# The state-space scan of a three-block layer stack: TensorE's order written out, decays two steps ahead, between-block decays from a table

## The chip, the cores and the metric

One core of one Trainium2 chip. The metric is the device time of one execution in microseconds (us); a kernel's time is the median over its runs. Engines are called TensorE (PE, with its weight loads PEld), VectorE (DVE), ScalarE (ACT), GpSimd (POOL) and SyncE (SP, which issues nearly all DMAs).

## The reference, cut to what matters

256 tokens, 1024 features, float32. A first block (a recurrent mixer, forgetting attention, a 16-expert feed-forward) is followed by two layers, each of a feed-forward, a mixer and a second feed-forward. The mixer has three parts whose outputs go side by side through one output projection: a state-space part (16 heads of 64, both directions, chunks of 128), latent attention (8 heads), and a gated convolution. The change is in the state-space part. For one direction and chunk it is

```
seg     = a_cs[l] - a_cs[s]
decay   = exp(where(l >= s, seg, -inf))
cb      = C[l] . B[s]
y_diag  = sum_s cb[l,s] * decay[l,s,h] * xd[s,h]
y_off   = C[l] . state of the chunk before * exp(a_cs[l])
```

The sequence has two blocks of 128, so each direction has one "block before", and `exp(a_cs[l])` is what the change calls the decays between blocks.

## The kernel before, in words

Every float32 matrix product is done in three passes: each operand is split into a high part `hi` and a rest `lo`, and `mm3` issues hi x hi, hi x lo, lo x hi (L281, L282, L283). A weight chunk of 128x2048 is fetched by `load` (L260): SP issues the DMA into one of three `raw` buffers, ScalarE casts each half to `hi` (L273) and VectorE subtracts to get `lo` (L274); there are five `hi` and five `lo` buffers of 128x1024. All of a load's instructions are given a priority 300 instructions earlier than their place. `add_to_X` (L315, L317) adds a finished 128x512 product to the residual X on VectorE, with a priority 500 earlier.

The order of the instructions on each engine is settled when the program is built: a planner takes, for each engine, the instruction of the highest priority that its own cost estimates say is ready; priority is program order, but for the two shifts above. On the chip each engine runs its list in that order and waits where an input or a buffer is late. TensorE's outputs go to eight PSUM banks of 128x512: four with the tag `acc`, four with the tag `wk`.

`_mix` (L1296) runs the mixer of a layer. Its last calls before the scan are the projection pieces `Z(2)` and `Z(3)`; between their halves a list `fill` puts other work: `ssd_operands` (two groups that transpose the inputs and multiply C with B), then `conv_tile` (four tiles: a `wk` bank with a broadcast row from TensorE L1468, VectorE `yn` L1471 out of that bank, ScalarE `oh` L1474, VectorE `ol` L1475). Then `ssd_scan` (L1579) runs. It has these pieces, named here as the change names them:

- D(i), `decay(i)`: for head pair i and each direction one `wk` bank, filled by a bf16 mask matmul (L1593) and two 256-column ones (L1597); four ScalarE exponentials of 128x128 per direction (L1603); VectorE adds the two directions (L1606) and multiplies by `cb` (L1608).
- O(i), `outputs(i)`: a `wk` bank with the between-block exponents (L1615) and a ScalarE exponential of it (L1618, tile `v`); a second `wk` bank for the outputs (L1623 from `xu` and `cb`, L1628 from `xt` and the decay tile `m`); six VectorE operations (L1630 to L1638, L1644) and two of ScalarE (L1637, and L1640 or L1643) that end in the two parts of an operand of the output projection.
- P(i), `project(i)`: twelve 512-column matmuls into the four `acc` banks; every second one begins with a load; P(3) and P(7) end a group of four with a norm (`rsqrt`, whose power runs on GpSimd) and four `add_to_X`.
- C and M, `project_others`: the convolution's and the attention's rows of the output projection, in two calls each. A call is a load and two tiles of twelve 512-column matmuls, each tile in a bank of its own (`acc` for C, `wk` for M) and each with an `add_to_X`.
- N, `head_norm`, and H, `head_T`: the norm of the attention output, and its transposes, four `wk` banks with two transposes each (L1896).
- E, `enter(0)`: transposes of the finished first half of X for the next feed-forward (L326), called inside the last call of M.

Before the change the program order is a loop of ten rounds. Round i has D(i); in rounds 0 and 1 two C tiles each; N in round 1; O(i-1); H in round 4; the first two M tiles in round 9; P(i-2); the last two M tiles and E stand behind the loop. The planner may take TensorE's instructions out of this order. The program runs the scan twice, once for each of the two layers.

Of the kernel before, what the change touches and what calls it, by code (L numbers as in the profile page):

```python
# [10 lines left out]
F32 = mybir.dt.float32  # L11
# [3 lines left out]
AF = mybir.ActivationFunctionType  # L15
# [4 lines left out]
P = 128  # L20
T = 256
TB = 2
D = 1024
# [9 lines left out]
WHOLE = "mmmmrrrmmmppppp"  # L33
EARLY = 13
SLOTS = 64

# [172 lines left out]
class Kern:  # L209
    def __init__(self, tc, ctx, io):  # L210
        self.tc, self.nc, self.ctx, self.io = tc, tc.nc, ctx, io
        nc = self.nc
        ep = lambda *a, **k: ctx.enter_context(tc.tile_pool(*a, **k))
        self.const = ep(name="const", bufs=1)
        self.res = ep(name="res", bufs=1)
        self.act = ep(name="act", bufs=1)
        self.wp = ep(name="wp", bufs=1)
        self.sm = ep(name="sm", bufs=3)
        self.ps = ep(name="ps", bufs=1, space=PSUM)
        self.X = [self.res.tile([P, D], F32, name=f"X{t}") for t in range(TB)]  # L220
# [8 lines left out]
        self.turn, self.nmore, self.slots, self.fine = 0, 0, [], False  # L229
# [31 lines left out]
    def load(self, ap, n=CH, sub=1024, eng=None):  # L261
# [14 lines left out]
                w.lo.append(lo)  # L276
        return w

    def mm3(self, out, ah, al, bh, bl, start, stop):
        nc = self.nc  # L280
        nc.tensor.matmul(out, ah, bh, start=start, stop=False)  # L281
        nc.tensor.matmul(out, ah, bl, start=False, stop=False)  # L282
        nc.tensor.matmul(out, al, bh, start=False, stop=stop)  # L283

    def rsqrt(self, out, ss, scale, n, pool=True):

# [31 lines left out]

    def half_T(self, h):

        nc = self.nc
        for k in range(4 * h, 4 * h + 4, 2):
            ps = self.bank()
            for t in range(TB):
                for j in range(2):
                    nc.tensor.transpose(ps[:, j * T + t * P:j * T + (t + 1) * P],  # L326
                                        self.X[t][:, (k + j) * P:(k + j + 1) * P], self.ident)
            yield k, ps

    def half_parts(self, h):  # L330
# [1221 lines left out]
    def ssd_operands(self, mp, S, xs):  # L1552

        nc = self.nc
        u = S["u"]
        xt = mp.tile([P, TB, 16, 64], F32, name="xt", tag="qT")
        xu = mp.tile([P, 2, 16, 64], F32, name="xu", tag="kT")
        cb = mp.tile([P, 2, 2, TB, P], F32, name="cb", tag="q")

        def group(g):  # L1560
            ps = self.bank()
            for t in range(TB):
                nc.tensor.matmul(ps[:, t * T:(t + 1) * T], xs[:, 8 + g, t * P:(t + 1) * P], xs[:, 10 + g],
# [4 lines left out]
            for t in range(TB):  # L1568
                ps = self.bank()
                for i in range(4):  # L1570
# [5 lines left out]
        S["xt"], S["xu"], S["cb"] = xt, xu, cb  # L1576
        return [lambda g=g: group(g) for g in range(2)]

    def ssd_scan(self, l, mp, S, xs, zs, wout, mla, cv):  # L1579
# [6 lines left out]
        def decay(i):  # L1586

            ms = []
            for d in range(2):
                tgt, src = S["tgt"][d], S["src"]  # L1590
                gp = self.bank()
                gv = gp.rearrange("p (a t) -> p a t", a=2)
                nc.tensor.matmul(gp, self.identb, self.maskb[d].unsqueeze(1).to_broadcast([P, 4, P]),  # L1593
                                 start=True, stop=False)
                for j in range(2):
                    e = self.esel[:, 2 * i + j:2 * i + j + 1].to_broadcast([P, P])
                    nc.tensor.matmul(gv[:, j], e, tgt, start=False, stop=j == 1)  # L1597
# [13 lines left out]

        def outputs(i, mv):
            g = i // 4
            vp = self.bank()
            nc.tensor.matmul(vp[:, :T], self.epair[:, 2 * i:2 * i + 2].rearrange("p a q -> p (a q)"), S["tx"],  # L1615
                             start=True, stop=True)
            v = self.t256(mp, "v")
            nc.scalar.activation(v, vp[:, :T], AF.Exp)  # L1618
            yp = self.bank()

            for d in range(2):
                s = slice(T + (1 - d) * P, T + (2 - d) * P)
                nc.tensor.matmul(yp[:, s], xu[:, d, 2 * i:2 * i + 2].rearrange("p a q -> p (a q)"),  # L1623
                                 cb[:, g, 1, d], start=True, stop=True)
            for j in range(2):
                for t in range(TB):
                    ts = slice(t * P, (t + 1) * P)
                    nc.tensor.matmul(yp[64 * j:64 * j + 64, ts], xt[:, t, 2 * i + j], mv[:, j, ts],  # L1628
                                     start=True, stop=True)
            nc.vector.tensor_tensor(v, yp[:, T:], v, op=OP.mult)  # L1630
            y = self.t256(mp, "y")
# [12 lines left out]
                nc.vector.tensor_tensor(ssq[:, g], sq, ssq[:, g], op=OP.add)  # L1644
            return hh, hl

        def project(i, hh, hl):
            g = i // 4
            if i % 4 == 0:
                S["acc"] = [[self.bank("acc") for _ in range(2)] for _ in range(TB)]  # L1650
            if i % 2 == 0:
# [4 lines left out]

            sp = self.bank()
            for t in range(TB):
                nc.tensor.matmul(sp[:, t:t + 1], ssq[:, g, t * P:(t + 1) * P], self.ones, start=True, stop=True)
# [5 lines left out]
        def project_others(c, ops, n, tag):  # L1665
            wt = self.load(wout[c + n])
            for t in range(TB):
                ps = self.bank(tag)
                if c and n == 1 and t == 1:
                    self.enter(0)  # L1670
                for i in range(4):
                    hh, hl = (a[:, t * P:(t + 1) * P] for a in ops[i])
                    self.mm3(ps, hh, hl, *wt(i * 512, 512), i == 0, i == 3)
                self.add_to_X(t, n, ps, 1.0)


        mv, ops = {}, {}
        for i in range(10):
            if i < 8:
                mv[i] = decay(i)  # L1680
            if i < 2:
                project_others(0, cv["ops"], i, "acc")
            if i == 1:
                self.head_norm(mp, mla["o"], 8, 64)
            if 0 <= i - 1 < 8:
                ops[i - 1] = outputs(i - 1, mv.pop(i - 1))
            if i == 4:
                mla["ops"] = self.head_T(mp, mla["o"], 8, 64, lambda i: self.col(f"o_norm{l}", i))
            if i == 9:
                project_others(6, mla["ops"], 0, "wk")  # L1690
            if i >= 2:
                project(i - 2, *ops.pop(i - 2))
        project_others(6, mla["ops"], 1, "wk")

    def rope(self, mp, dst, src, nh):

# [191 lines left out]
    def head_T(self, mp, o, nh, dh, gain):  # L1888
# [4 lines left out]
        for i in range(w // P):  # L1893
            ps = self.bank()
            for t in range(TB):
                nc.tensor.transpose(ps[:, t * P:(t + 1) * P],  # L1896
                                    o[:, t].rearrange("p h d -> p (h d)")[:, i * P:(i + 1) * P], self.ident)
            hh, hl = self.parts(mp)
            g = gain(i)
# [52 lines left out]
```

## Time and profile before

| what | value |
|---|---|
| runs, median of 3 | 1595.91 us (1593.9 to 1596.26) |
| the profiled execution | 1596.67 us, of which 1594.9 us are the span of its trace |
| first scan, from its first decay matmul to the next stage's first matmul | 740.28 to 812.3 us |
| second scan, likewise | 1331.92 to 1404.76 us |

How to read it: the span is what the profiler's instructions cover, and about 1.8 us of the execution lie around it. Times of rows are microseconds from the span's start. A row of a timeline is start, duration, engine, line, operation, output<-inputs, and in brackets the idle time of the engine just before it and what ended that. Successive matmuls overlap in their durations, so the distance between two starts is what one costs.

### The profile page before, as it was taken

To read this page: it belongs to the slowest core of one execution; us is meant where nothing else is said; L and a number is where in the kernel's file an instruction comes from. 1 tells how busy PE (TensorE), PEld (TensorE's weight loads), DVE (VectorE), ACT (ScalarE), POOL (GpSimd) and SP (SyncE) were. 2 spreads that over 40 slices of the span, in tenths; PEclk is the share of its full clock that TensorE was granted. 3 is DMA by queue.
4 is the path that set the end of the run, shared out by engine and by line. 5 is a ranking of instruction groups with operands and counts; after the bars stand their busy time and mean duration, and the time that the engine had idled before them with its cause. 6 is when DMAs were issued, how large, how long until landed. Compare 5 with 4: busy or idle time off the path is not lost.

```text
span 1594.9 us, 23124 instructions
## 1 busy us (share of the span) xinstructions
PE 1540.8 (97%) x8907; PEld 1247.7 (78%) x8907; DVE 1085.1 (68%) x1857; ACT 813.6 (51%) x1488; POOL 74.7 (5%) x97
## 2 busy tenths in 40 slices
PE   8999799988899999999899999999999999999999
PEld 7988444433788888998688888888889998788887
DVE  5977312112766778989977666767678989886675
ACT  5544211112655557666665555655567666565553
POOL 0320000000000001210000000000000210000000
PEclk9999899999999999999999999999999999999999
DMA  9534599999855125333245454555445333245552
GB/s 379 236 107 159 208 414 417 417 417 419 333 183 205 60 100 188 137 133 116 96 160 190 179 208 171 176 206 190 171 172 185 133 127 112 93 173 184 202 190 85
DMA packets 50085, 320.21 MB, mean 201 GB/s; under 512 B 5808, under 2 KB 6064, under 8 KB 16048
## 3 DMA queue, kind: packets, MB, share of 16 engines
q1 hardware_dynamic: 49392, 318.05, 53.0%
q8 instruction: 73, 1.20, 0.3%
q10 hardware_dynamic: 576, 0.60, 0.1%
q14 instruction: 44, 0.36, 0.1%
HBM read 317.58 MB, written 1.05 MB: 200 GB/s over the span
## 4 chain that ended last, share of the span: by engine, by line
PE 70%; DMA 9%; DVE 6%; ACT 2%; issue 1%; POOL 0%; DVEq 0%; ACTq 0%; SPq 0%; POOLq 0%
PE wk L1276 20%; PE wk L1277 10%; PE acc L281 9%; PE acc L282 9%; PE acc L283 9%; PE wk L1035 4%; DMA more<-in_wmoe_dram 3%; DMA whole<-in_wmoe_dram 3%; DMA raw<-in_wmoe_dram 2%; DVE lo L274 2%; PE acc L1035 1%; DVE xs L1409 1%; PE acc L1276 1%; PE wk L281 1%; PE wk L1832 1%
## 5 line engine op out<-in xcount | busy, mean ns | idle before, releaser
L274 DVE TENSOR_TENSOR lo<-raw,hi 128x1024 fp32r<-128x1024 f32 (+1 forms) x338 | 408.9, 1220 | 166.7 <-ACT hi L273 166.1
L1276 PE MATMUL wk<-x,hi 128*128 128x512 f32 x1344 | 473.6, 397 | 0.2 <-DVE gu L419 0.2
L273 ACT CAST hi<-raw 128x1024 fp32r<-128x1024 f32 (+1 forms) x338 | 349.1, 1043 | 232.3 <-PE wk L1276 133.5
L1277 PE MATMUL wk<-x,lo 128*128 128x256 f32 x1344 | 375.3, 279 | 0.0
L1276 PEld LDWEIGHTS wk<-x,hi 128*128 128x128 f32 x1344 | 252.9, 188 | 60.6 <-issue 0.6
L1277 PEld LDWEIGHTS wk<-x,lo 128*128 128x128 f32 x1344 | 253.8, 189 | 1.6
L281 PE MATMUL acc<-x,hi 128*128 128x256 f32 x640 | 186.7, 292 | 0.0
L283 PE MATMUL acc<-x,lo 128*128 128x256 f32 x640 | 181.3, 283 | 2.5 <-DVE lo L274 2.5
L282 PE MATMUL acc<-x,hi 128*128 128x256 f32 x640 | 181.1, 283 | 0.0
L281 PE MATMUL acc<-hi,hh 128*128 128x512 f32 x352 | 139.1, 395 | 3.8 <-ACT hh L427 3.8
L283 PE MATMUL acc<-hi,hl 128*128 128x512 f32 x352 | 138.8, 394 | 0.0
L282 PE MATMUL acc<-lo,hh 128*128 128x512 f32 x352 | 138.8, 394 | 0.0
L283 PEld LDWEIGHTS acc<-x,lo 128*128 128x128 f32 x640 | 122.1, 191 | 3.1 <-DVE lo L274 2.9
L281 PEld LDWEIGHTS acc<-x,hi 128*128 128x128 f32 x640 | 122.1, 191 | 2.7 <-issue 1.7
L282 PEld LDWEIGHTS acc<-x,hi 128*128 128x128 f32 x640 | 122.2, 191 | 0.5
L274 DVE TENSOR_TENSOR lo<-more,hi 128x1024 fp32r<-128x1024 f32 x72 | 91.6, 1283 | 40.3 <-ACT hi L273 40.1
L273 ACT CAST hi<-more 128x1024 fp32r<-128x1024 f32 x72 | 74.3, 1047 | 40.8 <-PE wk L1276 30.7
L281 PEld LDWEIGHTS acc<-hi,hh 128*128 128x128 f32 x352 | 66.2, 188 | 19.5 <-ACT hh L427 4.0
L422 ACT ACTIVATE sg<-gu 128x256 f32<-128x256 f32 x88 | 36.5, 415 | 87.2 <-DVE gu L420 87.1
L283 PEld LDWEIGHTS acc<-hi,hl 128*128 128x128 f32 x352 | 66.2, 188 | 15.6
L282 PEld LDWEIGHTS acc<-lo,hh 128*128 128x128 f32 x352 | 66.2, 188 | 13.8
L1035 PE MATMUL wk<-more,xg 128*64 128x512 f32 x256 | 74.6, 598 | 1.8 <-DMA more<-in_wmoe_dram 1.8
(433 smaller groups left out, 2370.6 us busy)
## 6 DMA issues: line engine op xcount, KB each, us to landing
raw<-in_ffn_dram SPq DMA_DIRECT2D x109, 1024.0 KB, 4.8
more<-in_wmoe_dram SPq DMA_DIRECT2D x48, 1024.0 KB, 13.8
raw<-in_win_dram SPq DMA_DIRECT2D x35, 1024.0 KB, 4.8
whole<-in_wmoe_dram SPq DMA_DIRECT2D x54, 512.0 KB, 12.0
more<-in_ffn_dram SPq DMA_DIRECT2D x23, 1024.0 KB, 8.2
raw<-in_wmoe_dram SPq DMA_DIRECT2D x21, 1024.0 KB, 16.2
raw<-in_wout_dram SPq DMA_DIRECT2D x18, 1024.0 KB, 4.9
more<-in_win_dram SPq DMA_DIRECT2D x9, 1024.0 KB, 17.0
```

The source lines that it names most:

```text
L273: nc.scalar.copy(hi[:, :sub], raw[:, s])
L274: (eng or nc.vector).tensor_tensor(lo[:, :sub], raw[:, s], hi[:, :sub].bitcast(F32), op=OP.subtract)
L281: nc.tensor.matmul(out, ah, bh, start=start, stop=False)
L282: nc.tensor.matmul(out, ah, bl, start=False, stop=False)
L283: nc.tensor.matmul(out, al, bh, start=False, stop=stop)
L422: nc.scalar.activation(sg, gu[:, 0], AF.Silu)
L1035: self.tc.keep_in_program_order(nc.tensor.matmul(*a, **k))
L1276: nc.tensor.matmul(ps, hi, self.both[k], start=k == 0, stop=False)
L1277: nc.tensor.matmul(ps[:, :T], lo, self.both[k][:, :T], start=False, stop=k == KT - 1)
L1409: nc.vector.scalar_tensor_tensor(o, xp[:, j, q:q + T], cwh[:, 12 * q + i:12 * q + i + 1], o, op0=OP.mult, op1=OP.add)
L1832: nc.tensor.matmul(ps[:, j * 96:(j + 1) * 96], pt[:, i * P:(i + 1) * P], v[:, s, (h + j) * 65:(h + j) * 65 + 96], start=s == 0, stop=s == 1)
```

## The change

The scan's pieces are run in the order of a string, and TensorE keeps that order: `mm` and `tr` mark their instruction so that the planner may not take it out of program order while `inorder` is set, which is from the string's first piece to its last. The decay matmuls stand two steps ahead of the outputs that use them (the tile `m0` gets three buffers of its own), the C and M tiles stand singly between the steps, and the between-block exponentials move out of `outputs` into `ssd_operands`: two head pairs share a bank and one 128x512 exponential, and the results stay in a table `vt` of 128x2048.

```
+SCAN = "D0 C0 D1 C1 N0 D2 O0 C2 D3 O1 C3 D4 O2 P0 D5 O3 P1 D6 O4 H0 P2 D7 O5 P3 O6 M0 O7 M1 P4 P5 P6 P7 M2 E0 M3"
...
+    def mm(self, *a, **k):
+        ins = self.nc.tensor.matmul(*a, **k)
+        if self.inorder:
+            self.tc.keep_in_program_order(ins)
...
+        vt = mp.tile([P, 4, 512], F32, name="vt")
         def group(g):
+            for q in (2 * g, 2 * g + 1):
+                ps = self.bank()
+                for i in range(2):
+                    e = self.epair[:, 4 * q + 2 * i:4 * q + 2 * i + 2].rearrange("p a q -> p (a q)")
+                    nc.tensor.matmul(ps[:, i * T:(i + 1) * T], e, S["tx"], start=True, stop=True)
+                nc.scalar.activation(vt[:, q], ps, AF.Exp)
...
-                m = self.t512(mp, f"m{d}")
+                m = self.t512(mp, "m1") if d else mp.tile([P, 512], F32, name="m0", bufs=3)
...
-            vp = self.bank()
-            nc.tensor.matmul(vp[:, :T], self.epair[:, 2 * i:2 * i + 2].rearrange("p a q -> p (a q)"), S["tx"],
-                             start=True, stop=True)
-            v = self.t256(mp, "v")
-            nc.scalar.activation(v, vp[:, :T], AF.Exp)
+            v = S["vt"][:, i // 2, i % 2 * T:(i % 2 + 1) * T]
...
+        def other(c, src, tag, k):
+            n, t = divmod(k, 2)
+            if t == 0:
+                S["wo"] = self.load(wout[c + n])
+            ps = self.bank(tag)
+            for i in range(4):
+                hh, hl = (a[:, t * P:(t + 1) * P] for a in src["ops"][i])
+                self.mm3(ps, hh, hl, *S["wo"](i * 512, 512), i == 0, i == 3)
+            self.add_to_X(t, n, ps, 1.0)
...
+        self.inorder = True
+        for step in SCAN.split():
+            do[step[0]](int(step[1]))
+        self.inorder = False
```

`mm3`, the transposes of `half_T` and `head_T`, and the scan's own matmuls now go through `mm` and `tr`. Loads, ScalarE, VectorE and GpSimd are still ordered by the planner.

## Rows read from the trace of the kernel before

**Rows 1.** The page: busy time of each engine; the chain that ended last.
```profile
PE 1540.8 (97%) x8907; PEld 1247.7 (78%) x8907; DVE 1085.1 (68%) x1857; ACT 813.6 (51%) x1488; POOL 74.7 (5%) x97
PE 70%; DMA 9%; DVE 6%; ACT 2%; issue 1%; POOL 0%; DVEq 0%; ACTq 0%; SPq 0%; POOLq 0%
```

**Rows 2.** Windows: length, busy PE, PEld, DVE, ACT, POOL; clock, DMA share, GB/s.
```profile
740.28:787.50 47.22, 42.23 (x249) 32.52 (x248) 43.07 (x90) 35.26 (x99) 1.08 (x1) 1.00 0.28 94
787.50:812.30 24.80, 24.80 (x122) 20.31 (x122) 20.82 (x38) 13.79 (x26) 0.69 (x1) 1.00 0.35 128
1331.92:1379.10 47.18, 42.60 (x241) 32.88 (x242) 43.02 (x89) 34.55 (x98) 1.08 (x1) 0.97 0.26 93
1379.10:1404.76 25.66, 25.66 (x129) 20.98 (x130) 20.93 (x38) 14.36 (x28) 0.69 (x1) 0.99 0.34 124
740.28:805.40 65.12, 60.13 (x335) 47.15 (x335) 57.92 (x116) 43.50 (x112) 1.08 (x1) 1.00 0.29 101
725.00:735.00 10.00, 10.00 (x82) 9.77 (x81) 9.60 (x21) 5.02 (x11) 0.00 (x0) 1.00 0.31 107
```

**Rows 3.** TensorE's waits, first scan: total us, times, longest.
```profile
PE wk L1623 <- ACT m L1603: 2.4, 3, 1.1
...
PE wk L1628 <- DVE m L1608: 0.7, 2, 0.4
...
PE wk L1593 <- ACT m L1603: 0.3, 1, 0.3
```

**Rows 4.** TensorE's timeline at H and the next P.
```profile
769.66 0.44 PE L1896 MATMUL wk<-cf,o 128*128 128x128 f32 x2 [0.42 <-ACT m L1603]
771.06 0.50 PE L281 MATMUL acc<-hi,x 128*128 128x512 f32 x1 [0.96 <-ACT x L1637]
```

**Rows 5.** Windows of the second scan, columns as in rows 2.
```profile
1372.00:1376.00 4.00, 2.20 (x15) 1.51 (x15) 4.00 (x7) 3.24 (x11) 0.00 (x0) 1.00 0.12 49
1376.00:1380.00 4.00, 4.00 (x25) 3.18 (x26) 3.60 (x9) 2.92 (x11) 0.00 (x0) 0.57 0.00 0
```

**Rows 6.** Groups by line and shape, first scan: busy us, mean ns.
```profile
L1615 PE MATMUL wk<-rows,epair 128*128 128x256 f32 x8 | 2.3, 293 | 0.0
L1618 ACT ACTIVATE v<-wk 128x256 f32<-128x256 f32 x8 | 3.1, 388 | 0.0
L1361 ACT ACTIVATE zth<-zs 128x512 f32<-128x512 f32 x1 | 0.6, 627 | 0.0
```

**Rows 7.** TensorE's timeline where the first scan begins.
```profile
738.95 0.64 PE L1468 MATMUL wk<-cvrow,epair 128*128 128x256 f32 x4
740.28 0.38 PE L1593 MATMUL wk<-mask_low,identb 128*128 128x512 bf16 x1 [0.70 <-DVE yn L1471]
...
741.00 0.50 PE L281 MATMUL acc<-hi,oh 128*128 128x512 f32 x1
...
742.27 0.39 PE L1593 MATMUL wk<-mask_excl,identb 128*128 128x512 bf16 x1
```

**Rows 8.** VectorE's timeline, same place.
```profile
739.76 0.47 DVE L1471 SCALAR_TENSOR_TENSOR yn<-cvy,colt,wk 128x256 f32<-128x256 f32 x1
740.15 1.23 DVE L274 TENSOR_TENSOR lo<-raw,hi 128x1024 fp32r<-128x1024 f32 x1
...
741.63 1.26 DVE L1471 SCALAR_TENSOR_TENSOR yn<-cvy,colt,wk 128x256 f32<-128x256 f32 x3
...
744.58 0.42 DVE L1475 TENSOR_TENSOR ol<-yn,oh 128x256 fp32r<-128x256 f32 x1
```

**Rows 9.** VectorE's timeline: the last weight part of the first scan.
```profile
804.22 1.22 DVE L274 TENSOR_TENSOR lo<-raw,hi 128x1024 fp32r<-128x1024 f32 x1
```

**Rows 10.** TensorE's timeline: a matmul of M(2), third operand.
```profile
807.44 0.40 PE L282 MATMUL wk<-lo,oh 128*128 128x512 f32 x1
```

**Rows 11.** Waits of all engines, 738.95 to 812.3 us: total us, times, longest.
```profile
ACT hi L273 <- PE acc L283: 14.4, 11, 2.6
DVE lo L274 <- ACT hi L273: 4.2, 7, 1.1
```

More of the change, by code (lines that the diff above doesn't have):

```diff
@@ L277, in load, with tr @@
         return w
+    def mm(self, *a, **k):
+        ins = self.nc.tensor.matmul(*a, **k)
+        if self.inorder:
+            self.tc.keep_in_program_order(ins)
+    def tr(self, *a):
+        ins = self.nc.tensor.transpose(*a)
+        if self.inorder:
+            self.tc.keep_in_program_order(ins)
     def mm3(self, out, ah, al, bh, bl, start, stop):
[L280 to L283, printed above, removed]
+        self.mm(out, ah, bh, start=start, stop=False)
+        self.mm(out, ah, bl, start=False, stop=False)
+        self.mm(out, al, bh, start=False, stop=stop)
     def rsqrt(self, out, ss, scale, n, pool=True):
@@ L319, in half_T @@
     def half_T(self, h):
-        nc = self.nc
         for k in range(4 * h, 4 * h + 4, 2):
@@ L325, in half_T @@
                 for j in range(2):
-                    nc.tensor.transpose(ps[:, j * T + t * P:j * T + (t + 1) * P],
-                                        self.X[t][:, (k + j) * P:(k + j + 1) * P], self.ident)
+                    self.tr(ps[:, j * T + t * P:j * T + (t + 1) * P],
+                            self.X[t][:, (k + j) * P:(k + j + 1) * P], self.ident)
             yield k, ps
@@ L1592, in decay @@
                 gv = gp.rearrange("p (a t) -> p a t", a=2)
-                nc.tensor.matmul(gp, self.identb, self.maskb[d].unsqueeze(1).to_broadcast([P, 4, P]),
+                self.mm(gp, self.identb, self.maskb[d].unsqueeze(1).to_broadcast([P, 4, P]),
                                  start=True, stop=False)
@@ L1596, in decay @@
                     e = self.esel[:, 2 * i + j:2 * i + j + 1].to_broadcast([P, P])
-                    nc.tensor.matmul(gv[:, j], e, tgt, start=False, stop=j == 1)
-                m = self.t512(mp, f"m{d}")
+                    self.mm(gv[:, j], e, tgt, start=False, stop=j == 1)
+                m = self.t512(mp, "m1") if d else mp.tile([P, 512], F32, name="m0", bufs=3)
                 for j in range(2):
@@ L1627, in outputs @@
                     ts = slice(t * P, (t + 1) * P)
-                    nc.tensor.matmul(yp[64 * j:64 * j + 64, ts], xt[:, t, 2 * i + j], mv[:, j, ts],
+                    self.mm(yp[64 * j:64 * j + 64, ts], xt[:, t, 2 * i + j], mv[:, j, ts],
                                      start=True, stop=True)
@@ L1658, in project @@
             for t in range(TB):
-                nc.tensor.matmul(sp[:, t:t + 1], ssq[:, g, t * P:(t + 1) * P], self.ones, start=True, stop=True)
+                self.mm(sp[:, t:t + 1], ssq[:, g, t * P:(t + 1) * P], self.ones, start=True, stop=True)
             self.rsqrt(inv[:, g], sp[:, :TB], 1.0 / 512, TB)
@@ L1663, in project, with heads @@
                           lambda n, t: self.add_to_X(t, n, S["acc"][t][n], inv[:, g, t:t + 1]))
[L1665 to L1674, printed above, removed]
-        mv, ops = {}, {}
[L1678 to L1693, printed above, removed]
+        def other(c, src, tag, k):
[7 more added lines that the diff above has]
+            self.add_to_X(t, n, ps, 1.0)
+        def heads():
+            mla["ops"] = self.head_T(mp, mla["o"], 8, 64, lambda i: self.col(f"o_norm{l}", i))
+        mv, ops = {}, {}
+        do = dict(D=lambda i: mv.__setitem__(i, decay(i)), O=lambda i: ops.__setitem__(i, outputs(i, mv.pop(i))), P=project,
+                  C=lambda k: other(0, cv, "acc", k), M=lambda k: other(6, mla, "wk", k), H=lambda i: heads(),
+                  N=lambda i: self.head_norm(mp, mla["o"], 8, 64), E=self.enter)
+        self.inorder = True
+        for step in SCAN.split():
+            do[step[0]](int(step[1]))
+        self.inorder = False
     def rope(self, mp, dst, src, nh):
@@ L1895, in head_T @@
             for t in range(TB):
-                nc.tensor.transpose(ps[:, t * P:(t + 1) * P],
+                self.tr(ps[:, t * P:(t + 1) * P],
                                     o[:, t].rearrange("p h d -> p (h d)")[:, i * P:(i + 1) * P], self.ident)
```

9 lines of the change are left out of this document (5 added, 4 removed).

## The prediction

> **What bounds the kernel now.** I read the page first, for which engine holds the end: TensorE is busy 97% of the span and makes up 70% of the chain that ended last [rows 1]. So only time in which TensorE stands idle, or runs at a lower clock, is to be had by a change of order. Then I cut the two scans, the only place touched, out with the windows view [rows 2]. What the reader is to see there: in the first 47.22 us of the first scan TensorE is busy 42.23, and in the last 24.80 us it never stops. The whole idle time of that scan is 47.22 - 42.23 = 4.99 us, all in its first two thirds. VectorE in those two thirds is busy 43.07 of 47.22 us, 91%, more than TensorE; in the last third it has slack (20.82 of 24.80). The second scan has the same shape, and lasts 47.18 + 25.66 = 72.84 us against 72.02.
>
> The waits of TensorE say what the 4.99 us are [rows 3, 4]. The first output matmul L1623 waits 2.4 us for the decay exponentials. It doesn't read them: its inputs `xu` and `cb` are finished before the scan. What it lacks is a `wk` bank that they still read. Four such banks are too few for a D (two) and an O (two) one right behind the other. The mask matmul waits 0.3 us and a head transpose 0.42 us for the same reason. L1628 waits 0.7 us for the decay itself, and the third P 0.96 us for its operand. Sum: 2.4 + 0.3 + 0.42 + 0.7 + 0.96 = 4.78; 0.21 us are in smaller gaps.
>
> The second scan is 0.82 us longer for another reason [rows 5]. Between 1372 and 1376 us TensorE was busy 2.20 of 4 us, and in the next 4 us the granted clock averaged 0.57 (2.4 GHz before, close to 1.2 GHz then). The Trainium skill ("TensorE: Matmul & The Clock Gate", What's actually happening) says that the clock depends on how busy the array has recently been; this row agrees.
>
> So what the change can win at most is 4.99 + (4.99 + 0.82) = 10.8 us in both scans, 0.7% of the time.
>
> **The change part by part.**
>
> *The table.* Eight TensorE matmuls L1615 and eight ScalarE exponentials leave each scan; eight matmuls and four 128x512 exponentials come in before it. TensorE's work is the same on both sides: the stage they go to is full (busy 10.00 of 10 us [rows 2]), so it grows by what the scan loses. Net 0; bounds -0.4 and +0.5 us per scan, the latter if the two more banks that a group now takes make it wait as long as L1593 or L1896 did (0.3 to 0.42 us [rows 3, 4]). ScalarE pays 4 x 0.63 = 2.5 us for 3.1 [rows 6], where it is busy 5.02 of 10 [rows 2]: hidden. What the table buys is a bank: an O takes one, not two.
>
> *Decays two steps ahead, P two steps behind O, other tiles between.* D(i+2) and O(i) need three banks of four, and a tile of twelve matmuls stands between one O and the next D, so the bank waits (2.4 + 0.3 us) go. A decay has a whole step more to finish (0.7 goes), and P(0) stands behind O(2), so its operand is two steps old (0.96 goes). P(4) needs the four accumulators that P(3)'s adds release; the tiles M(0) and M(1) and two O stand between. Taken: all 4.99 us go but for the two new waits below; in the second scan also the 0.82 us of slow clock.
>
> *New wait at the start.* The four convolution tiles hold all four `wk` banks. D(0) takes its first when the first `yn` has read it (740.28), but its second only at 742.27, since VectorE puts a weight part (740.15, 1.23 us) ahead of the next `yn` [rows 7, 8]. Before, five matmuls of C filled that time, from 741.00. In the fixed order C(0) stands behind D(0)'s second bank, and with it everything on TensorE: 742.27 - 740.9 = about 1.35 us idle (740.9 is 0.1 us before the 741.00 of the first C matmul). C(0) then runs to about 745.3, and its last operand part starts at 744.58 and ends at 745.0 [rows 8]: just in time. Bounds 0 (VectorE does the `yn` first) and 2.4 us (the last part comes 1 us later too). I take 1.35, the row.
>
> *New wait at the heads.* H takes all four banks right behind D(6) and O(4), which hold three. Before, H waited 0.42 us and the P behind it 0.96 [rows 4], with more room. P(2) now stands behind H and can't fill in. Bounds 0 and 2 us; I take the row's sum, 1.38.
>
> *Queues.* SP's loads move with their pieces: M's first chunk is fetched ahead of P(4)'s, not behind it. That costs nothing while the `hi` buffers, not the DMA, hold the loads up: ScalarE's casts wait 14.4 us for TensorE to release a buffer [rows 11]. If that cover went, a cast would wait for a transfer instead; the DMA engines are busy 0.28 to 0.35 of the time there [rows 2], so transfers have room. GpSimd has one power per group, M(0) and M(1) stand behind it. Nothing else is moved past it.
>
> *VectorE.* Its work is unchanged, so it must do the same in less time. Up to the last weight part of the scan, which ends at about 805.4 us [rows 9], it is busy 57.92 of 65.12 us, 89% [rows 2]; TensorE uses that part at 807.4 [rows 10], 2.0 us later. At the 91% that VectorE reached in the first two thirds it would finish at 740.28 + 57.92 / 0.912 = 803.8, so the end could come 3.6 us earlier (807.4 - 803.8). That lies above what I forecast, but not by much.
>
> **The sum.** First scan 4.99 - 1.35 - 1.38 = 2.26 us; second 4.99 + 0.82 - 2.73 = 3.08. Together 5.3 us. Against the profiled execution (1594.9 us of span, 1596.67 in all) that is 1591.3; that execution lies 0.76 us above the median of the runs, so the forecast is 1595.91 - 5.3 = **1590.6 us**. Ends of the terms: both new waits at 0 give 1585.1; both at their upper bounds (4.4 us) and the table at +0.5 give 4.99 - 4.9 = 0.1 in the first scan and 0.9 in the second, 1594.9.
>
> **The rivals.**
> - *The clock falls at the start.* From 738.95 to 742.27 TensorE would be busy some 1.3 us of 3.3, less than the 2.20 of 4 that came before the slow clock [rows 5, 7]. Against it: in the first scan a similar patch brought no drop (clock 1.00 [rows 2]). Price 0.82 us in each scan: 1590.6 + 1.6 = 1592.2.
> - *VectorE becomes the bound.* For it: 91% where it already leads, and no work taken off it. At a share of 89%, as before, it ends at 805.4 and 2.0 us of slack are all that is won in a scan; at 88% it ends at 806.1, 1.3 us won. Twice that gives 1592 to 1593.3; I say 1593. The Trainium skill ("Perfetto Trace Analysis", Identifying the Most-Contended Engine) says to speed up the engine with the highest occupancy first, and counts occupancy as a fair measure for VectorE, not for TensorE. By that rule a change of TensorE's order helps little here.
> - *Slower: the fixed order starves VectorE.* A `hi` buffer is released only when TensorE has used it, ScalarE waits for that, VectorE for ScalarE (14.4 and 4.2 us [rows 11]). When TensorE may not take another piece, each of its waits is passed on to the next load, and VectorE's pauses come back as late operands. It decides from the share at which VectorE ends later than TensorE needs now, 57.92 / (807.4 - 740.28) = 86%; at 83% it ends at 810.1, 2.7 us late in each scan: 1601.3. Against it: D two ahead and P two behind leave VectorE work in hand.
> - *The change doesn't do what it says*: the waits stay because the planner's VectorE order undoes them. 1595.9.
>
> **How the numbers follow.** The forecast as summed 0.40; the clock 0.18; VectorE the bound 0.22; starved 0.12; no effect 0.08. About 0.2%, 3.2 us, is what a measurement of this kernel can tell from no change, so the border of faster is 1592.7. The forecast's own spread (1585.1 to 1594.9) puts five sixths of it below that; the clock case three fifths; VectorE's two fifths: 0.33 + 0.11 + 0.09 = 0.53, and I say 0.55 faster. Starved and a little of the rest is slower, 0.12; same 0.33. The range leaves out the last parts at both ends: from 1586.5 (new waits of 0.7 us a scan) to 1598.0 (half of the starved case).
>
> **What would show it.** In the changed kernel's waits, L1623 should no longer wait for the exponentials, nor a P for its operand; the scan should last 69 to 70 us from the first decay matmul. The start should show a decay matmul that waits over 1 us for `yn`, and H waits for banks. The clock between D(0) and C(1) settles the first rival, VectorE's share up to the last weight part the second and third: over 90% and TensorE waiting for operands means the second, below 86% the third. I am wrong if TensorE idles 5 us or more in a scan, wherever that is, or if the stage before the scan grows by more than the 1 us of matmuls moved into it.

## The result, and the profile after

The changed kernel is **slower**: 1612.12 us median (1609.2 to 1617.15, 4 runs) against 1594.91 us for the kernel before in the same session, a ratio of 1.0111 [1.0078, 1.0143], some 17 us. The profiled execution took 1617.15 us (span 1615.3), the one before 1596.67 us: 20.5 us more. The profiled execution is the slowest of the four, which took 1609.20, 1609.27, 1614.98 and 1617.15 us at mean granted clocks of 0.990, 0.992, 0.986 and 0.984.

The page's busy time of each engine and the chain that ended last, changed kernel (before: [rows 1]):

```profile
PE 1552.6 (96%) x8907; PEld 1255.9 (78%) x8907; DVE 1085.1 (67%) x1857; ACT 813.0 (50%) x1480; POOL 75.3 (5%) x97
...
PE 66%; DMA 10%; DVE 8%; ACT 3%; issue 1%; POOL 1%; SPq 0%; ACTq 0%; DVEq 0%; POOLq 0%
```

VectorE's work is the same to 0.1 us. TensorE, with as many instructions, is busy 11.8 us longer, which more work can't explain. The windows view of the changed kernel, from the first decay matmul to the first matmul of the next stage, then three stretches of the first scan (columns as in [rows 2]):

```profile
739.97:821.22 81.25, 71.90 (x361) 55.53 (x360) 64.39 (x126) 46.35 (x116) 1.91 (x2) 0.92 0.26 92
1341.60:1425.10 83.50, 74.29 (x359) 57.35 (x359) 64.28 (x125) 46.14 (x116) 1.91 (x2) 0.88 0.25 89
762.50:767.40 4.90, 4.74 (x13) 3.32 (x14) 4.42 (x12) 0.31 (x2) 0.00 (x0) 0.65 0.30 119
779.20:783.50 4.30, 4.30 (x14) 3.05 (x14) 3.10 (x9) 1.29 (x3) 0.00 (x0) 0.64 0.01 4
808.70:814.70 6.00, 5.96 (x16) 4.89 (x17) 2.41 (x4) 1.45 (x4) 0.69 (x1) 0.51 0.53 176
```

The scans lasted 72.02 and 72.84 us [rows 2]; now 81.25 and 83.50. These +9.2 and +10.7 us make 19.9 of the 20.5, so the loss lies in the scans alone. The first scan has 81.25 - 71.90 = 9.35 us of idle TensorE time where it had 4.99, and three stretches in which the granted clock averages 0.65, 0.64 and 0.51: in the last one TensorE runs almost throughout at 1.2 GHz, not 2.4. What these stretches cost, worked out as length times (1 - clock), is 1.7 + 1.5 + 2.9 = 6.2 us (an estimate). With the 4.4 us of added idle time that makes 10.6; the table's eight matmuls, 1.3 us, have left the scan, and 9.2 remain. By the mean clocks of the two scan rows, 0.92 and 0.88, the lower clock costs some 6.5 us in the first scan and 10.0 in the second (length times 0.08 and 0.12, estimates too).

TensorE's waits in the first scan of the changed kernel (total us, times, longest; before: [rows 3, 4]), and below them its timeline at P(0), at H and at P(7)'s norm:

```profile
PE wk L282 <- DVE ssq L1657: 3.2, 1, 3.2
PE wk L287 <- DVE y L1645: 2.1, 2, 1.9
PE acc L282 <- ACT x L1650: 1.7, 1, 1.7
PE wk L282 <- ACT m L1620: 1.2, 1, 1.2
PE wk L287 <- ACT m L1620: 0.9, 1, 0.9
```

```profile
762.56 0.50 PE L282 MATMUL acc<-hi,x 128*128 128x512 f32 x1 [1.72 <-ACT x L1650]
...
775.75 0.44 PE L287 MATMUL wk<-cf,o 128*128 128x128 f32 x2 [0.91 <-ACT m L1620]
776.39 0.83 PE L287 MATMUL wk<-cf,o 128*128 128x128 f32 x4 [0.20 <-DVE y L1645]
779.08 0.41 PE L287 MATMUL wk<-cf,o 128*128 128x128 f32 x2 [1.86 <-DVE y L1645]
...
808.74 1.02 PE L282 MATMUL wk<-ones,ssq 128*128 128x1 f32 x4 [3.18 <-DVE ssq L1657]
```

The bank waits of the output matmuls are gone, as intended. In their place stand P(0), which waits 1.72 us for O(0)'s operand (L1650); H, which waits 0.91 + 0.20 + 1.86 us for banks; and P(7)'s norm, 3.18 us for the squares of O(7) (L1657). Each of the three slow stretches begins at one of these waits. The 1.2 us in the list stand at the start, ahead of D(0)'s second bank, and the clock behind them is 1.00 from 739.97 to 761.00 us. The second scan has the same waits at its start, but there the clock fell, as its timeline shows:

```profile
1343.44 0.41 PE L282 MATMUL wk<-mask_excl,identb 128*128 128x512 bf16 x1 [1.23 <-ACT m L1620]
...
1344.50 0.63 PE L282 MATMUL acc<-lo,oh 128*128 128x512 f32 x1
1344.93 0.63 PE L282 MATMUL acc<-hi,ol 128*128 128x512 f32 x1
...
1347.30 0.39 PE L282 MATMUL acc<-hi,ol 128*128 128x512 f32 x1
1347.53 0.39 PE L282 MATMUL acc<-hi,oh 128*128 128x512 f32 x1
```

The starts are first 0.43 us apart, then 0.23. The granted clock averages 0.50 from 1344 to 1346 us and 0.74 from 1346 to 1348, which costs 1.5 us by the same working.

VectorE's timeline shows why O(0) is late, a decay two steps ahead of its use notwithstanding:

```profile
755.31 0.41 DVE L1643 TENSOR_TENSOR vt<-wk,vt 128x256 f32<-128x256 f32 x1
...
755.72 0.47 DVE L1645 SCALAR_TENSOR_TENSOR y<-xs,colt,wk 128x256 f32<-128x256 f32 x1
...
757.36 0.42 DVE L1646 TENSOR_TENSOR y<-y,vt 128x256 f32<-128x256 f32 x1
...
758.59 1.22 DVE L275 TENSOR_TENSOR lo<-raw,hi 128x1024 fp32r<-128x1024 f32 x1
759.73 0.68 DVE L326 TENSOR_TENSOR X<-acc,X 128x512 f32<-128x512 f32 x1
760.33 1.21 DVE L275 TENSOR_TENSOR lo<-raw,hi 128x1024 fp32r<-128x1024 f32 x1
...
761.55 0.42 DVE L1647 SCALAR_TENSOR_TENSOR y<-y,zs 128x256 f32<-128x256 f32 x1
```

Four operations of O(0), 1.72 us of work, take from 755.31 to 761.97, since a decay's addition and product, two weight parts, an addition to X and small operations of the norms stand among them. From 750.00 to 762.50 us VectorE is busy 11.98 of 12.50 us: ahead of P(0) it has no time left. And when TensorE stands still, the loads do too. The waits of ScalarE and VectorE, same scan (before: 14.4 and 4.2 us [rows 11]):

```profile
ACT hi L274 <- PE acc L282: 16.4, 9, 4.7
DVE lo L275 <- ACT hi L274: 6.9, 7, 2.5
```

VectorE's timeline between P(0) and H shows two of these waits, and the operation that gives H its last bank (O(4)'s, which reads a `wk` bank):

```profile
768.64 1.23 DVE L275 TENSOR_TENSOR lo<-raw,hi 128x1024 fp32r<-128x1024 f32 x1 [1.72 <-ACT hi L274]
...
773.99 1.23 DVE L275 TENSOR_TENSOR lo<-raw,hi 128x1024 fp32r<-128x1024 f32 x1 [0.80 <-ACT hi L274]
...
778.46 0.47 DVE L1645 SCALAR_TENSOR_TENSOR y<-xs,colt,wk 128x256 f32<-128x256 f32 x1
```

The cast that the first low part waits for had itself waited 4.74 us for P(0) to release a buffer. Here VectorE is not short of time (busy 13.05 of 17.00 us from 768 to 785): it stands 2.5 us at low parts, with the outputs' operations behind them in its list. So P(0)'s wait fits too much work on VectorE, and H's wait fits P(0)'s lateness passed on through the loads.

### The profile page after: what moved, and what is told of

It reads as the page before. It is cut to its first block, busy times and chain, and to the rows that moved or that the text cites. A ratio compares the mean times of both kernels' runs of the same rounds, so it can differ in the third digit from the quotient of the medians.

```text
span 1615.3 us, 23111 instructions
## 1 busy us (share of the span) xinstructions
PE 1552.6 (96%) x8907; PEld 1255.9 (78%) x8907; DVE 1085.1 (67%) x1857; ACT 813.0 (50%) x1480; POOL 75.3 (5%) x97
## 4 chain that ended last, share of the span: by engine, by line
PE 66%; DMA 10%; DVE 8%; ACT 3%; issue 1%; POOL 1%; SPq 0%; ACTq 0%; DVEq 0%; POOLq 0%
PE acc L282 25%; PE wk L1286 19%; PE wk L1287 10%; DMA whole<-in_wmoe_dram 4%; PE wk L282 4%; DMA more<-in_wmoe_dram 3%; PE wk L1045 3%; DVE lo L275 3%; DMA raw<-in_wmoe_dram 2%; DVE xs L1419 2%; ACT hi L274 1%; PE acc L1286 1%; PE acc L1045 1%; PE wk L1841 1%; PE wk L1822 0%
## 5 line engine op out<-in xcount | busy, mean ns | idle before, releaser
L282 PE MATMUL acc<-x,hi 128*128 128x256 f32 x1280 | 239.2, 287 | 0.0
L282 PEld LDWEIGHTS acc<-x,hi 128*128 128x128 f32 x1280 | 200.2, 191 | 3.2 <-issue 1.7
L282 PE MATMUL acc<-hi,x 128*128 128x512 f32 (+1 forms) x352 | 125.3, 424 | 6.4 <-ACT x L1650 3.4
L282 PEld LDWEIGHTS acc<-hi,x 128*128 128x128 f32 x352 | 71.2, 205 | 23.4 <-ACT x L1650 3.9
```

The source lines that it names most:

```text
L282: ins = self.nc.tensor.matmul(*a, **k)
```

## The experiments

Each ratio is to the kernel before in the same session (1595.5 to 1596.9 us).

### Which part of the change costs

**Three buffers for the decay, alone (e7).**

```diff
-                m = self.t512(mp, f"m{d}")
+                m = self.t512(mp, "m1") if d else mp.tile([P, 512], F32, name="m0", bufs=3)
```

> The kernel before with the three own buffers for a decay tile alone (no table, order free, old loop). If the loss of e2 is the table's: 1594 to 1598 us. If it is the buffers': 1602 to 1607 us.

Measured: 1596.25 us, 1.0002 [0.9993, 1.0012]. The buffers are worth nothing.

**The table alone, in the kernel before (e6); then with each O keeping its old matmul, bank and exponential beside it, unused (e9).**

```diff
+            for q in (2 * g, 2 * g + 1):
...
+                nc.scalar.activation(vt[:, q], ps, AF.Exp)
...
-            vp = self.bank()
-            nc.tensor.matmul(vp[:, :T], self.epair[:, 2 * i:2 * i + 2].rearrange("p a q -> p (a q)"), S["tx"],
-                             start=True, stop=True)
-            v = self.t256(mp, "v")
-            nc.scalar.activation(v, vp[:, :T], AF.Exp)
+            v = S["vt"][:, i // 2, i % 2 * T:(i % 2 + 1) * T]
```

> The kernel before with the table alone (order free, old loop, old buffers of the decay tiles). If the loss of e2 (8 us) is the table's, since an O now takes one bank and decays run further ahead of O's: 1602 to 1607 us. If it is the buffers': 1594 to 1598 us.

Measured: 1604.73 us, 1.006 [1.0043, 1.0077].

> The kernel before with the table, and with the old matmul, bank and exponential of each O kept as well, their result unused. So the table's own work is there (1 us of matmuls per scan), but an O still takes two banks. If the table costs 9 us (e6) because an O that takes one bank lets the planner lay other lists: 1595 to 1600 us. If its work ahead of the scan costs that: 1603 us or more.

Measured: 1596.79 us, 1.0011 [1.0000, 1.0022]. The kernel with *more* work is 8 us faster than the one with less. So the table costs hardly anything where it is made; what costs about 9 us is that an O in the planner's free order no longer takes a bank, a matmul and an exponential of its own. Which of the three steers the planner was not separated. What it leads to is seen in TensorE's waits, table alone, first scan, where [rows 4] had 0.96 us for the same operand:

```profile
PE acc L281 <- ACT x L1641: 4.5, 2, 2.7
```

**The changed kernel without the table (e12)** (its O's own matmul and exponential in the fixed order).

```diff
-            v = S["vt"][:, i // 2, i % 2 * T:(i % 2 + 1) * T]
+            vp = self.bank()
+            self.mm(vp[:, :T], self.epair[:, 2 * i:2 * i + 2].rearrange("p a q -> p (a q)"), S["tx"],
+                    start=True, stop=True)
...
+            nc.scalar.activation(v, vp[:, :T], AF.Exp)
```

> The changed kernel without the table: each O has its matmul, its second bank and its exponential again, in the fixed order. Theory D: VectorE's work is the same, so 1605 to 1620 us. If the table is at fault here as in e6: 1600 to 1605 us.

Measured: 1609.78 us, 1.0097 [1.0080, 1.0114]. In a fixed order, which the planner can't rearrange, the table makes no difference that these runs can tell (1.0111 with it).

**The order free, or fixed, in the old or the new sequence** (table and buffers in all of them). The first edit alone is the new sequence free (e1); both edits are the old sequence free (e2); the second alone is the old sequence fixed (e3).

```diff
-        self.inorder = True
+        self.inorder = False
```

> The changed kernel with its string, its table and its three decay buffers, but TensorE's instructions not held in program order. Theory A (VectorE's list): an O's VectorE operations stand behind weight parts whose buffers TensorE has not yet released; TensorE may now take other work in such a wait, so most of the 9 us of idle time per scan goes: 1590 to 1600 us. Theory B (the fixed order as such costs, whatever VectorE does): 1595 us or less, a full return. Theory C (it is the new program order, decays ahead and tiles between, that is bad, whoever orders TensorE): still 1605 us or more.

```diff
-SCAN = "D0 C0 D1 C1 N0 D2 O0 C2 D3 O1 C3 D4 O2 P0 D5 O3 P1 D6 O4 H0 P2 D7 O5 P3 O6 M0 O7 M1 P4 P5 P6 P7 M2 E0 M3"
+SCAN = "D0 C0 C1 D1 C2 C3 N0 O0 D2 O1 P0 D3 O2 P1 D4 O3 H0 P2 D5 O4 P3 D6 O5 P4 D7 O6 P5 O7 P6 M0 M1 P7 M2 E0 M3"
```

> The order of before (a string that repeats the old loop) and TensorE free, so of the change only the table and the three buffers for one decay tile are left. All theories: within 3 us of the kernel before, 1592 to 1598 us. A clear gain or loss would be the table's own.

> The order of before, now held on TensorE. Theory A: the weight parts still come 300 instructions early, so O's operands are late here too, and with P only one step behind O more so: 1605 to 1625 us. Theory B: likewise slower than before, 1605 us or more. Theory C: about the time of before, 1593 to 1600 us, since the order is the old one.

Measured: new sequence free 1601.89 us, 1.0033 [1.0020, 1.0045]; old sequence free 1605.25, 1.0051 [1.0034, 1.0068]; old sequence fixed 1611.35, 1.0093 [1.0076, 1.0110]. Fixing costs 10 us in the new sequence and 6 in the old one, and once it is done the two sequences come out alike (1611 and 1612). Free, the new sequence is some 3 us ahead, with intervals that overlap. Of the expectations only e3's holds: e1 lies between the ranges of two theories, and e2 is 7 us above its range, which e6 and e9 put down to the table. Along one path from before to after: table +9, sequence -3, fixing +10, buffers 0.

### Why the fixed order loses

**The outputs' VectorE and ScalarE operations put ahead of the rest (e4).**

```diff
+            with self.urgent():
-            nc.vector.tensor_tensor(v, yp[:, T:], v, op=OP.mult)
+                nc.vector.tensor_tensor(v, yp[:, T:], v, op=OP.mult)
...
```

> The changed kernel with one thing more: the VectorE and ScalarE operations of an O get the priority of the additions to X, 500 instructions earlier, so they stand ahead of weight parts. Theory A: TensorE's waits for an O's operands (1.7, 1.9 and 3.2 us in a scan) and the slow clock behind them go, and the time falls to 1587 to 1597 us. Theory B: the fixed order still finds something late; 1605 us or more. Theory C: little change, 1605 us or more.

Measured: 1615.37 us, 1.0122 [1.0105, 1.0139]. The theory that the operands are late by a wrong priority falls. TensorE's waits of that run, both scans:

```profile
PE wk L282 <- DVE m L1625: 11.9, 4, 3.2
PE wk L287 <- DVE o L1892: 8.2, 4, 3.7
```

The operands of P no longer wait; the decays do (L1625) and the heads (L1892). What is hurried on VectorE makes something else late by as much.

**The scan's loads without their low parts: 18 us less for VectorE in each scan, in the changed kernel (e5) and in the one before (e13).** The matmuls read the high part in place of the low one, so as many matmuls run.

```diff
-                (eng or nc.vector).tensor_tensor(lo[:, :sub], raw[:, s], hi[:, :sub].bitcast(F32), op=OP.subtract)
+                if self.inorder:
+                    lo = hi
+                else:
+                    (eng or nc.vector).tensor_tensor(lo[:, :sub], raw[:, s], hi[:, :sub].bitcast(F32), op=OP.subtract)
```

> The changed kernel, but the loads inside the scan don't compute the low part of their weights; the matmuls read the high part in its place (so the scan's projections leave out what the low parts would add). VectorE has 16 subtractions of 1.13 us less in each scan, 18 us. Theory D (VectorE's amount of work ahead of each P is the bound): the waits for O's operands vanish and the time falls to 1592 us or less. Theory E (it is the lists that the planner lays for VectorE and ScalarE, casts that wait for a buffer ahead of what TensorE needs, not the amount): waits stay, 1600 us or more.

> The kernel before, with the loads of the scan computing no low part (the high part is read in its place, so the low parts' share of the three projections is left out): 15 subtractions of 1.22 us, 18 us of VectorE's work less in each scan. The control for the same edit in the changed kernel, which gave 1583.9 us. If the old order really cost TensorE the idle time that the prediction counted, and VectorE alone kept the new order from winning it, the old order keeps its bank waits (L1623 2.4 us, the mask 0.3, a head 0.4 per scan) and loses only the third P's wait of 1.0 us and the later slow clock: 1592 to 1595, and the changed kernel beats it by 8 to 11 us once VectorE has room. If the relief of VectorE is worth the same to any order, it comes to 1583 to 1586, and the new order has no merit of its own.

Measured: changed kernel 1583.86 us, 0.9935 [0.9919, 0.9952]; kernel before 1589.24 us, 0.9963 [0.9949, 0.9977]. The first scan of the one and of the other:

```profile
738.67:804.60 65.93, 65.10 (x360) 51.42 (x360) 51.33 (x114) 45.55 (x116) 1.56 (x2) 1.00 0.32 112
```

```profile
737.51:806.68 69.17, 66.94 (x368) 52.77 (x368) 51.78 (x114) 48.45 (x124) 1.39 (x2) 1.00 0.31 107
```

This is the main result. With room on VectorE the new order leaves 65.93 - 65.10 = 0.83 us idle and the clock is 1.00 in both scans; the same relief took 28 us off the changed kernel and 6 to 7 off the old one. The old order's first scan keeps 2.23 us idle: its waits for banks (1.8 and 0.3 us) stay, and those for a decay and for a P's operand are gone. So more than half of the 4.99 us that TensorE stood idle before goes with VectorE's relief alone, without a new order. With the same relief the change (order, table and buffers together) is worth some 5 us (5.4 by the medians, 0.28% or 4.5 us by the ratios, whose intervals overlap at their edges); the old order's 1589.24 us lies between the two outcomes that were expected. Two reservations. Leaving a low part out also brings each load to TensorE one operation earlier; but no wait of TensorE in the changed kernel's first scan ends with a weight part, so that can hardly be the gain. And it takes away not only VectorE's 18 us of work but also the 6.9 us for which VectorE stands at low parts that come too early in its list. Ahead of P(0) VectorE is busy almost throughout, so there it is the amount; behind P(0) no run here parts the amount from the place in the list.

**Filler on TensorE in the waits (e8)**: 7 unused mask matmuls ahead of P(0), 4 in each of two head groups, 13 ahead of P(7)'s norm.

```diff
+    def filler(self, ps, n):
+        for _ in range(n):
+            self.mm(ps, self.identb, self.maskb[0].unsqueeze(1).to_broadcast([P, 4, P]), start=True, stop=True)
```

> The changed kernel with extra bf16 mask matmuls of 0.23 us that nothing reads, where TensorE waits: 7 ahead of P(0), 4 ahead of the first and of the third head transposes, 13 ahead of the norm of P(7), each into a bank that the next real matmul starts over. They take about the time of the waits (1.7, 2.9, 3.2 us). Theory F (the lowered clock behind these waits costs some 6 us in each scan of the profiled run): the P behind them run at full clock and the time falls by 6 to 12 us, to 1600 to 1606 us. If the clock is not kept up by them, or costs little: 1610 us or more.

Measured: 1603.04 us, 1.0054 [1.0037, 1.0071]. The windows of that run around the three places:

```profile
761.00:768.00 7.00, 6.70 (x38) 4.49 (x36) 7.00 (x20) 4.41 (x13) 0.00 (x0) 1.00 0.29 118
775.00:785.00 10.00, 9.21 (x53) 7.21 (x52) 8.28 (x20) 5.97 (x17) 1.22 (x1) 1.00 0.17 55
803.00:815.00 12.00, 11.64 (x58) 9.01 (x56) 8.42 (x14) 6.27 (x15) 0.69 (x1) 1.00 0.25 88
```

The clock is 1.00 where it was 0.65, 0.64 and 0.51, and matmuls that compute nothing make the kernel 9 us faster. By the medians about half of the 17 us is the clock behind the waits, not the waits; the intervals of the two ratios leave anything from 3 to 15 us. The waits stay, filled: the first 512-column matmul of P(0) starts 3.9 us behind D(4)'s first with and without the filler. With the clock kept, the scans last 75.13 and 75.11 us, 3.1 and 2.3 us longer than before the change.

### VectorE's work moved to GpSimd

**The decay's two operations, in the changed kernel (e10), in the one before (e11), and in the free new order (e16).**

```diff
-            nc.vector.tensor_tensor(m, m, ms[1], op=OP.add)
+            nc.gpsimd.tensor_tensor(m, m, ms[1], op=OP.add)
...
-            nc.vector.tensor_tensor(mv, mv, cb[:, i // 4, 0].rearrange("p b q -> p (b q)").unsqueeze(1).to_broadcast([P, 2, T]),
+            nc.gpsimd.tensor_tensor(mv, mv, cb[:, i // 4, 0].rearrange("p b q -> p (b q)").unsqueeze(1).to_broadcast([P, 2, T]),
```

> The changed kernel with the sum of a decay's two directions and its product with cb on GpSimd in place of VectorE: 16 operations of 0.6 us less on VectorE in each scan (9.6 us, about half of what e5 took away); GpSimd needs 1.2 to 1.9 us for each by the rows of before for 128x512, and decays have two steps of time. Theory D (VectorE's amount): 1584 to 1597 us. Theory E (the lists): 1603 us or more. If GpSimd is too slow, the output matmuls wait for its decays, and that shows.

> The same move of the decay's two operations to GpSimd, in the kernel before. Theory D: VectorE's relief helps here too, but a decay has only one step of time, so some of it comes back as waits for decays: 1588 to 1599 us. If the fixed order with decays two steps ahead is what lets GpSimd be used, this one is slower than e10 by 3 us or more.

> The spread order left free to the planner (alone: 1601.9 us) with the decay's two operations on GpSimd. If the free order was already fitted to VectorE's pace, as in the kernel before, where this move gave 1596.4 against 1595.6, nothing is won: 1600 to 1604. If the spread order loses in both forms because VectorE has too much ahead of each P, it falls by some us, 1592 to 1598, and the amount of VectorE's work decides for free orders too.

Measured: 1603.49 us, 1.0055 [1.0039, 1.0072]; before 1596.42, 1.0007 [0.9998, 1.0017]; free new order 1597.64, 1.0008 [0.9998, 1.0018].

**The same with filler in the heads (e14); the second low part of each load of the scan on GpSimd (e15); both moves together, in the fixed (e17) and in the free order (e18).** The edit for the low parts:

```diff
+                if self.inorder and a:
+                    eng = nc.gpsimd
```

> The changed kernel with the decay's addition and its product with cb on GpSimd (alone: 1603.5 us) and eight filler matmuls in the head transposes, where that run still waits 2.9 and 2.3 us per scan and its granted clock is 0.90 between 768 and 785 us. If what is left there is half the wait and half the slow clock behind it, the filler, which runs within the waits, brings the clock back and some 2 to 3 us per scan: 1597 to 1599. If the waits alone count, it stays at 1602 to 1605.

> The changed kernel with the second low part of each load of the scan computed on GpSimd, not on VectorE: 7 or 8 subtractions of 1.22 us, about 9 us, off VectorE in each scan, as much as the decay's operations that went to GpSimd in an earlier run, but off the loads rather than off the way from a decay to its output. If it is the amount of VectorE's work ahead of each P and bank that decides, it falls as far as that run did or further, 1595 to 1604. If a load that takes longer (GpSimd took 1.4 to 1.5 us for half the elements, so about 2.9 us for one of these, an estimate) holds its hi buffer longer and TensorE behind it, it rises: 1610 to 1625.

> The changed kernel with both moves to GpSimd together: the decay's two operations (alone 1603.5 us) and the second low part of a load in the scan (alone 1606.0 us). That takes some 16 to 17 us of VectorE's work off each scan, nearly the 18 us whose removal gave 1583.9, with nothing left out; GpSimd then has about 23 + 15.5 us in a scan of 75. If the amount of VectorE's work ahead of each P and bank decides, the two gains of 9 and 6 us add up to 1595 to 1599, and if the low parts' slower way is no matter, to less. If what GpSimd takes longer for (2.6 us for a low part, 1.4 and 1.5 us for the decay's) is the new lateness, or its two kinds of work stand in each other's way, it stays at 1602 to 1608.

> The same two moves with the spread order left free to the planner (with the decay's operations alone on GpSimd: 1597.6 us against 1596.0 for the kernel before). If VectorE's amount of work still holds this order up, the second move gives some us more: 1590 to 1595, faster than the kernel before. If the free order has no more to win, or the low parts come too late from GpSimd, 1597 to 1603.

Measured: filler 1602.17 us, 1.0043 [1.0026, 1.0060]; low parts 1605.97, 1.0062 [1.0046, 1.0079]; both moves 1614.86, 1.0114 [1.0097, 1.0131]; both, free, 1607.88, 1.0068 [1.0052, 1.0085]. The filler missed its place: in the first scan the two longest waits, 2.3 us ahead of a decay and over 2 us between two of H's transposes, remain, and the window from 768 to 785 us shows a clock of 0.90 with and without it. The low parts alone came out between the two ranges that were expected. The sum of the two moves missed worse: gains of 9 and 6 us on the changed kernel became none, and in the free order the second move cost 10 us. Groups of VectorE's instructions in the scan, first of the changed kernel, then of both moves together (busy us, mean ns):

```profile
L328 DVE SCALAR_TENSOR_TENSOR X<-acc,ginv,X 128x512 f32<-128x512 f32 x8 | 5.7, 748 | 3.3 <-PE acc L282 2.7 <-POOL ginv L302 0.6
...
L1651 DVE SCALAR_TENSOR_TENSOR x<-y,colt,x 128x256 fp32r<-128x256 f32 x8 | 3.8, 477 | 0.2 <-ACT x L1650 0.2
...
L1647 DVE SCALAR_TENSOR_TENSOR y<-y,zs 128x256 f32<-128x256 f32 x8 | 3.3, 416 | 0.1
...
L1891 DVE TENSOR_TENSOR o<-o,oinv 128x512 f32<-128x512 f32 x2 | 1.3, 681 | 0.0
```

```profile
L1653 DVE SCALAR_TENSOR_TENSOR x<-y,colt,x 128x256 fp32r<-128x256 f32 x8 | 6.6, 826 | 1.7 <-ACT x L1652 1.7
L1649 DVE SCALAR_TENSOR_TENSOR y<-y,zs 128x256 f32<-128x256 f32 x8 | 6.1, 767 | 0.1
...
L330 DVE SCALAR_TENSOR_TENSOR X<-acc,ginv,X 128x512 f32<-128x512 f32 x8 | 5.5, 744 | 1.4 <-POOL ginv L304 1.4
...
L1893 DVE TENSOR_TENSOR o<-o,oinv 128x512 f32<-128x512 f32 x2 | 3.9, 1966 | 0.0
```

VectorE operations with both tensors in SBUF got longer while GpSimd worked (416 to 767 ns, 477 to 826, 681 to 1966); the one that takes a tensor from a PSUM accumulator did not (748 and 744). So what VectorE handed over came back as longer operations. The first scan with the decay's operations moved, and with both moves:

```profile
739.90:814.55 74.65, 66.70 (x361) 52.64 (x361) 63.86 (x110) 45.88 (x116) 25.26 (x18) 0.98 0.28 99
```

```profile
742.41:822.37 79.96, 71.45 (x360) 55.08 (x360) 65.37 (x104) 45.35 (x116) 39.78 (x24) 0.91 0.27 97
```

With 16 and 22 operations fewer (11.0 us, and 6 x 1.22 = 7.3 more), VectorE's 64.39 us should have become 53.4 and 46.1; they are 63.86 and 65.37. The Trainium skill ("SBUF — State Buffer", SBUF: two separate sides) says that a VectorE operation with two SBUF inputs and a GpSimd operation that reads SBUF lock each other out for a whole instruction; these rows agree. It follows that these runs do not test the theory that VectorE has too much to do, as they were meant to. The first move alone still returned 9 us. Most of that is the clock by the two scan rows: TensorE's idle time falls only from 9.35 to 7.95 us, its busy time from 71.90 to 66.70, at a clock of 0.98 against 0.92. P(0) no longer waits and P(7)'s norm waits 0.5 us, while H waits longer; why the waits fell so is open. No version tried beats the kernel before with all of its work done; the free new order with the decay on GpSimd equals it.

## Why the prediction was wrong

- **The step that failed** is the one on VectorE: "At the 91% that VectorE reached in the first two thirds it would finish at" 803.8, "so the end could come 3.6 us earlier". That is a sum over the whole scan, held against the scan's end. A fixed order needs VectorE's results at each P, H and norm, in TensorE's sequence. Up to 761.00 us, just ahead of P(0), VectorE was busy 18.72 of 21.03 us, 89%, the share that it had before, and O(0)'s operand still came 1.72 us late. A free planner may put another piece ahead of such a matmul; in the fixed order TensorE stops, the `hi` buffers stay full, and VectorE then waits itself. Its share over the scan falls to 64.39 / 81.25 = 79%, up to the scan's last weight part to 57.10 / 67.99 = 84%.
- **The third rival is what happened**: the fixed order starves VectorE, share below 86%, TensorE idle over 5 us. I gave it 0.12, against it "D two ahead and P two behind leave VectorE work in hand". Work in hand there was; ahead of P(0) what was missing is time to do it. Its price, 2.7 us in each scan, held no clock: it is near the 3.1 and 2.3 us that the scans are longer when filler keeps the clock up, and far below the 9.2 and 10.7 us measured without.
- **The clock** was priced by one event, "0.82 us in each scan", at the start. That rival came true in one scan of the two: at the start the clock stayed at 1.00 in the first (739.97 to 761.00) and fell in the second, for 1.5 us. In both it fell behind later waits, which no term held: 6.2 us in the first scan by the windows, and 9 us for both scans by the filler run.
- **"What the table buys is a bank"**, net 0: right as to its work (the stage before it ends at 739.97 us, was 740.28; and 1596.8 us with O's own work kept), wrong as to what the bank did. In the free order an O that claims less is laid differently by the planner, and that costs 9 us; in the changed kernel's fixed order it made no difference (1.0097 without the table, 1.0111 with it). I treated a claim on a bank as a cost only.
- **The new waits**: the start, 1.35 us forecast, measured 1.2, right in size. The view puts it down to D(0)'s exponentials (L1620) and not to `yn`; by the rows of their engines both end within 0.1 us of each other, so which of them held the bank is open. H, 1.38 us with 2 as the upper bound, measured 0.91 + 0.20 + 1.86 = 3.0. The waits at P(0) and at P(7)'s norm were not in the sum at all; I had P(0)'s as "two steps old" and so settled.
- **What was right**: the old output matmuls' bank waits go. With VectorE relieved, TensorE idles 0.83 us in a scan, and the change is worth about 5 us over the kernel before with the same relief, near the sum of 5.3. That nearness is partly luck: the relief alone takes 2.8 of the 4.99 us of idle time in the old order too, and the new wait of 1.35 us at the start isn't in the relieved kernel's list of waits. The sum was that of a machine in which VectorE is no limit. The range has a slip besides: half of the starved case's 5.4 us above 1595.91 is 1598.6, not 1598.0; the measured time lies beyond both.
- **The second rival's page**, the Trainium skill's "Perfetto Trace Analysis", Identifying the Most-Contended Engine, says to optimize the engine with the highest occupancy first. The runs agree: 18 us less on VectorE made even the old order 6 to 7 us faster, while the new order of TensorE alone lost 17.

## What to carry to other kernels

Before an engine's order is fixed, add up the other engines' work cumulatively at each point where the fixed order needs a result, not at the end of the stage: VectorE at 89% was late at three of them here. Price a new wait of 2 to 3 us on TensorE with the slow clock behind it, which here cost about as much as the waits. Claims on a shared buffer that look like a cost may be what keeps a free planner's order good, so take them away alone and measure before building on it.

## What the runs showed of the hardware

- Filler matmuls with unused results made the kernel 9 us faster, by a clock that stays at 1.00.
- The same waits on TensorE, 0.69 and 1.23 us at the start of a scan, left the granted clock at 1.00 in one scan and were followed by 0.50 and 0.74 in the other scan of the same execution.
- GpSimd's 128x512 operations and 128x1024 subtractions lengthened VectorE's operations on two SBUF tensors by 1.7 to 2.9 times, so that 18 us of work moved off VectorE in a scan left it as busy as before (65.37 us against 64.39).
